# A decoder layer on one Trainium2 core: one projection block earlier in the order, and weight stores on two other queues

## The chip, the cores and the metric

The kernel runs on one core of one Trainium2 chip. The time is that of one execution on the device, in microseconds (us). It is compared between kernels that run on the same chip.

## The reference

One decoder layer, 2048 tokens of width 1024, everything in float32:

```python
h = x @ w_in                       # columns split over three groups of heads
y = [GatedDeltaNet(4 heads of 128) | DilatedWindowAttn(4 heads of 64) | DiffAttn(4 heads)] @ w_out
x = LayerNorm(alpha * x + y)
f = W_down(silu(gate) * val),  [gate, val] = CausalDWConv3(x @ w_up)      # 2752 wide
x = LayerNorm(alpha * x + f)
```

GatedDeltaNet is a linear attention with a state that runs through the tokens in chunks. DilatedWindowAttn is a softmax over three windowed patterns (window 128 at step 1, 512 at step 4, 2048 at step 16), mixed by their log-sums. DiffAttn is full causal attention with two softmax maps, the second subtracted from the first.

## The kernel before, in words

**Products in halves.** TensorE multiplies float32 values as pairs of rounded numbers. Each operand is split into a high part (rounded to the fp32r format) and a low part (the rest), and a product is three matmuls: high by high, high by low, low by high (lines 206 to 208 for the projections, 1158 to 1161 for the products back to model width, 655 to 657 for the values). Moving operands are 512 tokens wide. The tokens are worked in four blocks of 512, numbered 0 to 3.

**Weights.** `Dense.weights` brings one weight tile of 128 by 1024 in two halves of 256 KB. A half that is met for the first time is loaded raw (line 151, tile `wraw`), rounded by ScalarE into `whi` (line 153), and POOL subtracts to get `wlo` (line 154). Where `keep` is set, the two parts of both halves are then stored to device memory (lines 157 to 161, `whi_d` and `wlo_d`), and later uses load those (line 148) and need neither ScalarE nor POOL. `keep` is set by job c0, so the weights of A3, o0 and block 0 of the feed-forward (f0) are stored; those of the gated projections are not. 85 weight tiles are kept: 12 in A3, 8 in o0, 65 in f0, each with four stores.

**Buffers for weights.** Until the end of the second list below, `wraw` has 6 buffers and `whi` and `wlo` 4 each. After it, all three share one ring of 14 tiles (`NW`), so that a raw half takes the slot that a half four or five before it has left.

**Jobs.** The program is written as three lists of jobs, and a job's number is a token block (in i, b, p and r a pair or half of blocks):

- A: projection for the two softmax groups (`Projection.project`: 8 products by `w_att`, then the values by `w_val`, twice over 4 weights; results go to device memory). G: projection for the gated group.
- i, b, p, r: the gated stage. i inverts triangular blocks, b merges them, p prepares keys and queries, r runs the recurrence over two chunks and stores its rows of `y_d`.
- w: dilated window attention of a block. d: differential attention of a block: `stats` (scores, minimum and sum, lines 767 to 776) and `weighted` (lines 818 to 843).
- c0: frees the gated projection's buffers and sets `keep`.
- o0: `Ffn.attend(0)`, the product of `y_d` by `w_out` for block 0 with the first LayerNorm. t0: `Ffn.turn`, which transposes its rows into the moving layout, 8 times 4 transposes (line 1175) and a split.
- f: the feed-forward of a block (`Ffn.block`: 43 products by `w_up`, convolution, products by `w_down`). Within it, attend and turn for the next block are done: attend(1) in f0, attend(2) in f1, attend(3) in f2. So attend(3) needs w3 and d3.

**Order.** A scheduler turns the program into one fixed order for each engine before the run. It simulates the run with a cost model, and each engine takes the ready instruction that stands first in the program. So the place of a job in the lists is its priority, and later jobs fill gaps as far as their buffers are free. On the chip each engine, and each engine's DMA queue, works through its fixed order: an instruction that waits holds up all behind it. Before the change all DMAs are begun on SyncE's queue (SP in the profile).

**Pools.** The second list works with the weight buffers `wp1`, three PSUM banks for products (two `psd`, one `psx`) and five banks of the gated stage; the third list's ring, two more product banks and the four banks for attention scores take the places that these leave. Each block's split tokens `xhi` and `xlo` have 8 buffers in all, one block's worth, so A2, A3 and t0 can't hold theirs at the same time.

Of the kernel before, what the change touches and what calls it, by code (L numbers as in the profile page):

```python
# [27 lines left out]
def cast(x):  # L28
    return x.bitcast(F32)
# [81 lines left out]
class Dense:  # L111
# [15 lines left out]
    def weights(self, src, k=KD, m=P, pool=None, key=None):  # L127


        nc = self.nc  # L130
        n = k // 2 * m
        shape = lambda w: w.rearrange("p (k m) -> p k m", k=k // 2)

        def put(dt, name):
            if pool:
                w = pool.tile([P, TB], dt, tag=name, name=name, bufs=12)
            elif self.ring:
                w = self.wp.tile([P, TB], dt, tag="w", name=name, bufs=self.ring)
            else:
                w = self.wp.tile([P, TB], dt, tag=name, name=name, bufs=NRAW if name == "wraw" else NHALF)  # L140
            return shape(w[:, 0:n])

        his, los = [], []
        for i in range(2):
            if key in self.kept:
                hi, lo = put(F32R, "whi"), put(F32R, "wlo")
                for part, d in zip((hi, lo), self.kept[key]):
                    nc.sync.dma_start(out=cast(part), in_=cast(shape(d[:, i * n : i * n + n])))
            else:
                raw = shape((self.wp.tile([P, TB], F32, tag="w" if self.ring else "wraw", name="wraw", bufs=self.ring or NRAW))[:, 0:n])  # L150
                nc.sync.dma_start(out=raw, in_=src[:, i * (k // 2) : (i + 1) * (k // 2)])
                hi, lo = put(F32R, "whi"), put(F32R, "wlo")
                nc.scalar.copy(hi, raw)  # L153
                nc.gpsimd.tensor_tensor(out=lo, in0=raw, in1=hi, op=ALU.subtract)  # L154
            his.append(hi)
            los.append(lo)
        if key is not None and self.keep and key not in self.kept:
            self.kept[key] = [self.tc.dram_tile([P, 1024], F32R, name=name) for name in ("whi_d", "wlo_d")]
            for parts, d in zip((his, los), self.kept[key]):
                for i in range(2):  # L160
                    nc.sync.dma_start(out=cast(shape(d[:, i * n : i * n + n])), in_=cast(parts[i]))
        return Halves(his), Halves(los)

    def split(self, raw, pool=None, tag="x", bufs=None):
# [1107 lines left out]
def decoder(tc, I, out, y_d=None, upto=3):  # L1272
    nc = tc.nc
    with ExitStack() as ctx:
# [49 lines left out]
        with ExitStack() as second:  # L1324
            dn.ps = Turns(psd, psd, second.enter_context(tc.tile_pool(name="psx", bufs=1, space=PSUM)))
            gdn_phase(tc, I, y_d, dn, gi, SECOND, emit)
        gates.close()
# [5 lines left out]
        ff.open(ctx)  # L1333
        for job in THIRD:
            if job == "f2":
# [36 lines left out]
NZ = 1  # L1372
LAG_PD = 2
FIRST = "A0 G0 A1 G1 d0 w0".split()
SECOND = "i0 b0 p0 b1 p1 r0 b2 p2 r1 G2 b3 p3 r2 G3 c0 i1 r3 p4 p5 b4 b5 r4 b6 r5 A3 p6 p7 b7 r6 r7 o0".split()
THIRD = "w1 d1 A2 t0 d2 w2 w3 d3 f0 f1 f2 f3".split()


def host_arrays(inputs):
# [75 lines left out]
```

## Time and profile before

| | |
|---|---|
| time, median of 3 runs | 3291.5 us (3281.3 to 3293.2) |
| profiled execution: time | 3290.28 us |
| its span | 3288.5 us |
| mean granted TensorE clock | 0.958 |
| device memory read, written | 500.82 MB, 155.39 MB (200 GB/s over the span) |
| stores of `whi_d` and `wlo_d` | 170 and 170, 256 KB each, on SyncE's queue |

The span runs from the first instruction to the last; the execution's own time has 1.8 us around it. In the profile PE is TensorE's matmuls, PEld its weight loads, DVE is VectorE, ACT ScalarE, POOL GpSimd, SP SyncE; a q behind the name is the engine's queue of waits and DMA issues. L161 is line 161 of the kernel. An arrow `out<-in` names the tile written and the tiles read. The granted clock is what the throttle left TensorE, as a share of full speed. The lines of the profile stand in the prediction, where they are used.

### The profile page before, as it was taken

What the parts mean: (1) busy time and instruction counts of PE and PEld (TensorE: products, weight loads), DVE (VectorE), ACT (ScalarE), POOL (GpSimd) and SP (SyncE); (2) the same over time, 40 slices, a digit from 0 to 9 for tenths busy, and PEclk for the clock granted to TensorE, in tenths of its full rate; (3) what the DMA queues carried; (4) which work ended last, traced back from release to release, by engine and by line L of the source; (5) the groups of instructions that cost most, each with busy time, mean ns of one, the idle gap of its engine ahead of it and who ended that gap; (6) DMA issues with size and microseconds to landing.
All of it is one profiled execution on the core that took longest, in us unless ns stands there. A gap on an engine that the chain in (4) does not pass through costs nothing.

```text
span 3288.5 us, 43511 instructions
## 1 busy us (share of the span) xinstructions
PE 3033.3 (92%) x14476; PEld 2318.8 (71%) x14476; DVE 1870.7 (57%) x3392; ACT 1354.4 (41%) x3188; POOL 660.0 (20%) x571
## 2 busy tenths in 40 slices
PE   7898989998597798898899899999999999999998
PEld 5676867786476675565656677778866668888887
DVE  2562759665346245656746675557884444474446
ACT  3653553644144134645744332235653432122213
POOL 4563545442230012242212200000000000000001
PEclk9999989999688898998999999999999999999999
DMA  6546364546797776666677676666874545776554
GB/s 207 168 141 213 121 211 138 156 138 209 247 306 249 240 242 201 199 205 209 203 226 235 215 251 198 183 183 195 261 220 154 162 142 189 243 240 194 192 186 147
DMA packets 474209, 659.29 MB, mean 200 GB/s; under 512 B 75169, under 2 KB 201633, under 8 KB 473217
## 3 DMA queue, kind: packets, MB, share of 16 engines
q1 hardware_dynamic: 473984, 656.52, 63.2%
q8 instruction: 115, 1.88, 0.2%
q14 instruction: 110, 0.89, 0.1%
HBM read 500.82 MB, written 155.39 MB: 200 GB/s over the span
## 4 chain that ended last, share of the span: by engine, by line
PE 56%; DMA 12%; ACT 4%; DVE 3%; issue 2%; SPq 2%; POOL 1%; ACTq 0%; POOLq 0%; DVEq 0%
PE d L208 9%; PE d L206 9%; PE d L207 9%; PE rp L1158 6%; PE rp L1159 6%; PE rp L1161 5%; DMA wraw<-in_w_up 5%; PE bank L818 3%; DMA wraw<-in_w_down 3%; PE bank L833 2%; ACT whi L153 2%; PE bank L997 1%; DMA ks<-fk_d 1%; PE bank L1004 1%; PE bank L767 1%
## 5 line engine op out<-in xcount | busy, mean ns | idle before, releaser
L206 PE MATMUL d<-xhi,whi 128*128 128x512 f32 x2144 | 865.6, 404 | 41.1 <-ACT whi L153 16.4
L208 PE MATMUL d<-xhi,wlo 128*128 128x512 f32 x2144 | 861.3, 402 | 27.8 <-DMA wlo<-wlo_d 14.4
L207 PE MATMUL d<-xlo,whi 128*128 128x512 f32 x2144 | 858.9, 401 | 1.1 <-DVE xlo L169 1.1
L154 POOL TENSOR_TENSOR wlo<-wraw,whi 128x512 fp32r<-128x512 f32 x370 | 504.1, 1367 | 1471.1 <-ACT whi L153 1331.5
L206 PEld LDWEIGHTS d<-xhi,whi 128*128 128x128 f32 x2144 | 412.9, 193 | 153.0 <-ACT whi L153 26.2
L208 PEld LDWEIGHTS d<-xhi,wlo 128*128 128x128 f32 x2144 | 412.0, 192 | 136.8 <-POOL wlo L154 23.3
L207 PEld LDWEIGHTS d<-xlo,whi 128*128 128x128 f32 x2144 | 412.7, 192 | 102.8 <-issue 17.8
L153 ACT CAST whi<-wraw 128x512 fp32r<-128x512 f32 x370 | 227.7, 618 | 390.8 <-DMA wraw<-in_w_up 118.5
L1159 PE MATMUL rp<-wlo,hhi 128*128 128x512 f32 x704 | 280.9, 400 | 2.0 <-POOL wlo L154 2.0
L1158 PE MATMUL rp<-whi,hhi 128*128 128x512 f32 x704 | 268.1, 402 | 12.9 <-ACT whi L153 11.9
L1161 PE MATMUL rp<-whi,hlo 128*128 128x512 f32 x672 | 263.7, 396 | 0.0
L776 ACT ACTIVATE bank<-bank,nm 128x512 f32<-128x512 f32 (+3 forms) x320 | 190.1, 594 | 100.9 <-DVE nm L772 65.2
L1090 ACT COPY ub<-d 128x512 f32<-128x512 f32 x172 | 100.8, 586 | 315.9 <-PE d L208 315.3
L772 DVE TENSOR_REDUCE nm<-bank 128x1 f32<-128x512 f32 (+3 forms) x288 | 164.7, 598 | 96.1 <-PE bank L767 89.6
L843 POOL TENSOR_SCALAR_AFFINE_SELECT pd<-pd 128x128 f32<-128x128 f32 x64 | 32.5, 512 | 854.9 <-DVE pd L839 851.1
L839 DVE SCALAR_TENSOR_TENSOR pd<-pe,f_nlam,pd 128x512 f32<-128x512 f32 (+3 forms) x160 | 124.0, 782 | 138.3 <-ACT pe L835 109.6
L1158 PEld LDWEIGHTS rp<-whi,hhi 128*128 128x128 f32 x704 | 131.7, 189 | 55.4 <-ACT whi L153 19.1
L1159 PEld LDWEIGHTS rp<-wlo,hhi 128*128 128x128 f32 x704 | 133.5, 190 | 39.2 <-issue 6.9
L365 DVE SCALAR_TENSOR_TENSOR yc<-ub,i_taps,yc 128x512 f32<-128x512 f32 x144 | 156.3, 1086 | 3.3
L1168 DVE TENSOR_TENSOR r<-r,rp 128x512 f32<-128x512 f32 x152 | 101.8, 684 | 91.5 <-PE rp L1161 87.0
L1161 PEld LDWEIGHTS rp<-whi,hlo 128*128 128x128 f32 x672 | 127.3, 189 | 31.2 <-issue 4.8
L818 PE MATMUL bank<-pd,fv 128*64 128x512 f32 (+3 forms) x320 | 143.4, 553 | 0.0
(281 smaller groups left out, 4545.7 us busy)
## 6 DMA issues: line engine op xcount, KB each, us to landing
whi<-whi_d SPq DMA_DIRECT2D x486, 256.0 KB
wlo<-wlo_d SPq DMA_DIRECT2D x486, 256.0 KB
whi_d<-whi SPq DMA_DIRECT2D x170, 256.0 KB
wlo_d<-wlo SPq DMA_DIRECT2D x170, 256.0 KB
wraw<-in_w_gdn SPq DMA_DIRECT2D x128, 256.0 KB
ks<-fk_d SPq DMA_DIRECT2D x160, 196.0 KB
wraw<-in_w_up SPq DMA_DIRECT2D x86, 256.0 KB
wraw<-in_w_down SPq DMA_DIRECT2D x50, 256.0 KB
```

What stands on the lines that cost most here:

```text
L153: nc.scalar.copy(hi, raw)
L154: nc.gpsimd.tensor_tensor(out=lo, in0=raw, in1=hi, op=ALU.subtract)
L206: nc.tensor.matmul(out=ps, lhsT=whi[:, k], rhs=xhi[k], start=(k == 0), stop=False)
L207: nc.tensor.matmul(out=ps, lhsT=whi[:, k], rhs=xlo[k], start=False, stop=False)
L208: nc.tensor.matmul(out=ps, lhsT=wlo[:, k], rhs=xhi[k], start=False, stop=(k == KD - 1))
L365: nc.vector.scalar_tensor_tensor(out=yc, in0=ub[:, j : j + TB], scalar=self.taps[:, mt, j : j + 1], in1=yc, op0=ALU.mult, op1=ALU.add)
L772: nc.vector.tensor_reduce(out=o, in_=s[:, 0:nf], axis=mybir.AxisListType.X, op=ALU.min)
L776: nc.scalar.activation(out=s[:, 0:n], in_=s[:, 0:n], func=AF.Exp, scale=-1.0, bias=o, accum_out=den[:, b, m, qt : qt + 1])
L818: nc.tensor.matmul(out=po[64 * hh : 64 * hh + 64, q0:], lhsT=v[:, 64 * hh : 64 * hh + 64], rhs=pd[hh][:, q0:], start=start, stop=stop)
L1158: nc.tensor.matmul(out=ps, lhsT=hi[:, sl], rhs=whi, start=first, stop=False)
L1159: nc.tensor.matmul(out=ps, lhsT=hi[:, sl], rhs=wlo, start=False, stop=last and lo is None)
L1161: nc.tensor.matmul(out=ps, lhsT=lo[:, sl], rhs=whi, start=False, stop=last)
```

## The change

Two edits. In `Dense.weights` the four stores of a kept weight are begun on other queues: the two of the high part on ScalarE's (`nc.scalar`), the two of the low part on POOL's (`nc.gpsimd`). In the lists, A2 moves from the third list, where it stood after w1 and d1, to the second, between r6 and r7; and t0 moves from the third list, where it stood behind A2, to the end of the second, right behind o0. A2 so uses the second list's weight buffers instead of the ring.

```diff
@@ -156,9 +156,9 @@
         if key is not None and self.keep and key not in self.kept:
             self.kept[key] = [self.tc.dram_tile([P, 1024], F32R, name=name) for name in ("whi_d", "wlo_d")]
-            for parts, d in zip((his, los), self.kept[key]):
+            for eng, parts, d in zip((nc.scalar, nc.gpsimd), (his, los), self.kept[key]):
                 for i in range(2):
-                    nc.sync.dma_start(out=cast(shape(d[:, i * n : i * n + n])), in_=cast(parts[i]))
+                    eng.dma_start(out=cast(shape(d[:, i * n : i * n + n])), in_=cast(parts[i]))
         return Halves(his), Halves(los)
@@ -1372,8 +1372,8 @@
 FIRST = "A0 G0 A1 G1 d0 w0".split()
-SECOND = "i0 b0 p0 b1 p1 r0 b2 p2 r1 G2 b3 p3 r2 G3 c0 i1 r3 p4 p5 b4 b5 r4 b6 r5 A3 p6 p7 b7 r6 r7 o0".split()
-THIRD = "w1 d1 A2 t0 d2 w2 w3 d3 f0 f1 f2 f3".split()
+SECOND = "i0 b0 p0 b1 p1 r0 b2 p2 r1 G2 b3 p3 r2 G3 c0 i1 r3 p4 p5 b4 b5 r4 b6 r5 A3 p6 p7 b7 r6 A2 r7 o0 t0".split()
+THIRD = "w1 d1 d2 w2 w3 d3 f0 f1 f2 f3".split()
```

## The prediction

> **What bounds the kernel now.** I read the page first, then the busy time by stages, then in the stage that looked held up the chain of waits and the two lists of waits, and last the timelines of the DMA queue and of TensorE around the moved blocks. The page:
>
> ```profile
> span 3288.5 us, 43511 instructions
> PE 3033.3 (92%) x14476; PEld 2318.8 (71%) x14476; DVE 1870.7 (57%) x3392; ACT 1354.4 (41%) x3188; POOL 660.0 (20%) x571
> ```
>
> TensorE is the bound by this row, but matmuls overlap, so busy says little about pace. The stages show it (us; then busy us and count of each engine, the granted clock, DMA share, GB/s):
>
> ```profile
> 820.00:920.00 100.00, 58.13 (x290) 43.72 (x291) 30.92 (x59) 19.65 (x37) 22.60 (x18) 0.68 0.80 262
> 920.00:1060.00 140.00, 118.09 (x949) 101.29 (x948) 81.47 (x170) 64.84 (x175) 30.03 (x27) 0.91 0.87 279
> 1060.00:1200.00 140.00, 112.69 (x585) 88.32 (x584) 44.17 (x124) 31.70 (x65) 4.63 (x4) 0.88 0.78 246
> 1200.00:1886.00 686.00, 626.32 (x2474) 420.65 (x2473) 418.74 (x764) 362.16 (x865) 194.70 (x164) 0.96 0.67 210
> 1886.00:2714.00 828.00, 824.18 (x3847) 609.63 (x3845) 517.40 (x996) 343.48 (x802) 9.04 (x18) 1.00 0.62 196
> 328.00:410.00 82.00, 81.85 (x435) 65.84 (x434) 58.90 (x95) 40.96 (x89) 42.56 (x34) 1.00 0.39 125
> 3034.00:3116.00 82.00, 82.00 (x363) 67.73 (x362) 37.91 (x57) 16.89 (x43) 0.00 (x0) 1.00 0.60 193
> ```
>
> The last row is the last block's feed-forward alone: 82/363 = 0.226 us for a matmul of 512 columns with nothing in the way. From 1886 on TensorE is full at clock 1.00, and nothing can be won there. The slow part is 820 to 1886: the end of the gated stage with A3 and o0 (to 1060), A2, w1 and t0 (to 1200), and f0 beside d1 and d2 (to 1886). In f0's 686 us, 2474 matmuls at 0.226 would take 559 us. One group is dearer than that price:
>
> ```profile
> L818 PE MATMUL bank<-pd,fv 128*64 128x512 f32 (+3 forms) x160 | 73.2, 554 | 0.0
> ```
>
> It holds TensorE for 73.2 us where 160 x 0.226 = 36 were counted, so the floor is at most 596 us, and about 90 us of f0 are lost. The chain of waits there repeats itself for long stretches (start, us, what):
>
> ```profile
> 1546.89 3.88 DMA wraw<-in_w_down
> ...
> 1550.85 0.63 ACT whi L153
> 1551.48 0.02 issue
> 1551.49 0.32 SPq L161
> 1551.81 0.05 issue
> 1551.86 4.97 DMA wraw<-in_w_down
> ```
>
> A weight half lands, ScalarE rounds it, SyncE's queue, which stood at the store of that half, issues the store, and only then the load of the next half. One load is in flight at a time. The lists of waits over the same 686 us (waiter, what it waited for, us, times, longest), SyncE's and ScalarE's:
>
> ```profile
> SPq L161 <- ACT whi L153: 215.4, 92, 4.5
> SPq L161 <- POOL wlo L154: 46.6, 81, 1.1
> ...
> ACT whi L153 <- DMA wraw<-in_w_up: 118.5, 58, 4.4
> ACT whi L153 <- DMA wraw<-in_w_down: 51.7, 27, 4.3
> ```
>
> 262 us of waiting in front of stores on SyncE, 170 us of ScalarE's waiting for loads. That this is the queue's order and not the weights' path itself, the casts of line 153 show, alone by stage:
>
> ```profile
> 328.00:410.00 82.00, 14.26 (x23) 1.00 0.39 125
> 1200.00:1886.00 686.00, 79.23 (x128) 0.96 0.67 210
> ```
>
> From 328 to 410 the same load, cast and subtract run beside w0, without stores: one half per 3.57 us, TensorE full. In f0 it is one per 5.36 us.
>
> **The stores.** Line 161 issues 4 stores of 256 KB for each kept weight: 12 weights in A3, 8 in o0, 65 in f0, so 340 in all, 260 of them in f0. The change gives 170 to ScalarE's queue and 170 to POOL's.
>
> ```profile
> L161 SPq DMA_DIRECT2D whi_d<-whi x170: 319/320/3069, 745.5 to 1879.6; - x170
> L154 POOL TENSOR_TENSOR wlo<-wraw,whi x370: 1250/1289/3551, 4.5 to 3247.7; 128x512 fp32r<-128x512 f32 x185
> ```
>
> SyncE loses 340 issues (min/median/max in ns, so 0.32 us by the median). In f0 it loses the 262 us of waits too, and the next load then waits only for a slot of the ring of 14 tiles, four halves ahead. ScalarE in f0 gains 130 x 0.32 = 42 us on 362 of 686; the store follows its own cast in program order, so it waits for nobody else, and what queues behind it are the exponentials of d1 and d2. The 170 us that ScalarE now waits for loads cover this; were they gone altogether it would still be busy only 404 of about 600 us. On POOL no DMA issue is in this trace. Bounds: 0.32 us, as on SyncE, and 3.55 us, the slowest POOL operation above. Nothing here lets an issue cost less than nothing. I take 1.3 us, a POOL operation's median: 2.6 us per half with the subtract, below the 3.57 of the rate without stores. The upper end gives 4.8 us per half, and f0 would gain little; both ends stay in the range.
>
> So f0 can gain from 0 to 90 us. The row 328:410 says nearly all, but there the DMA share was 0.39; f0 in 600 us would move 210 x 686/600 = 240 GB/s. I take 60.
>
> A rule of the Trainium skill speaks against this: "DMA: Bandwidth & Descriptors", section "Issuing engines are not separate DMA queues", says that starting DMAs from several engines saves only the sequencer's time of issue, which is usually small. By it f0 would gain one issue per half; the trace disagrees so far as 215 us of waiting stand in front of those issues. Where only issues are dense the rule fits.
>
> **A2 and t0.** A2 is 288 matmuls (65 us at 0.226), and its DMAs are 8 of x, 64 of kept halves and about 45 stores, some 25 MB. They move ahead of r7 and o0 on every queue (SyncE's, the matmuls, ScalarE's and VectorE's copies; POOL has only a memset of it), and no longer stand behind w1 and d1. t0's 32 transposes and 8 splits now follow o0. None of it is cheaper; what counts is which gaps it fills. r7's tail has gaps (TensorE's timeline, with the idle time before each):
>
> ```profile
> 1045.56 1.82 PE L557 MATMUL pk<-S,qk 128*128 128x128 f32 x8 [2.51 <-DVE on L582]
> 1055.22 2.07 PE L564 MATMUL pv<-R,g_xt 128*128 128x128 f32 x8 [7.84 <-DVE R L560]
> ...
> 1070.21 1.12 PE L598 MATMUL yp<-d_ident,on 128*128 128x128 f32 x4 [6.94 <-POOL on L595]
> ```
>
> 17 us in three gaps, which A2 or o0 could fill. But from 820 to 1200 the DMA engines are nearly full: 26.2 + 39.1 + 34.4 = 99.7 MB, which at 279 GB/s, the best stage above, still takes 357 of the 380 us. So this stretch, with its stores moved and its order changed, can gain at most 23 us. It can also lose: A2's 25 MB are 90 us at that rate, put ahead of r7, o0 and so of w1, and SyncE's queue is dense there. Such a stretch, with issues slowed to over a microsecond each by full queues:
>
> ```profile
> 876.43 4.45 SPq L700 DMA_DIRECT2D fk_d<-sy  x3
> 880.98 3.65 SPq L161 DMA_DIRECT2D whi_d<-whi  x2
> ```
>
> I bound it by +40 us lost (A2's 90 less what its own place at 1060 to 1200 frees) and 23 won, and take 20 won, since 80 of the 340 stores leave this queue just here.
>
> **What is late next.** Attention (w1, d1, d2, w2, w3, d3) is one chain of its own. SyncE's timeline gives first loads and last stores of d1, d2 and d3, and the first load of attend(3), which needs d3:
>
> ```profile
> 1273.34 0.86 SPq L741 DMA_DIRECT2D qs<-fq_d  x2
> 1504.63 0.32 SPq L869 DMA_DIRECT2D y_d<-ob  x1
> 1507.27 0.33 SPq L741 DMA_DIRECT2D qs<-fq_d  x1
> 1849.70 0.41 SPq L869 DMA_DIRECT2D y_d<-ob  x1
> 2187.08 0.33 SPq L741 DMA_DIRECT2D qs<-fq_d  x1
> 2713.98 0.32 SPq L869 DMA_DIRECT2D y_d<-ob  x1
> 2825.25 0.32 SPq L1149 DMA_DIRECT2D yraw<-y_d  x1
> ```
>
> d2 took 342 us for 3 key blocks (114 each), d3 527 for 4 (132 each) beside a full TensorE. The slack before attend(3) is 2825 - 2714 = 111 us. If f0 fills TensorE, d1 and d2 slow towards d3's pace; half of the difference, 9 us on 5 blocks, is 45. Then feed-forward can get ahead of attention by only 111 - 45 = 66 us, plus what w1 starts or runs earlier. That allows about 80 us in all, the size of my sum.
>
> **The sum.** 60 + 20 = 80 us from the profiled execution's 3290.3, which lies 1.2 us under the median 3291.5: 3210 us. A difference under 0.5% (16 us) I count as none.
>
> **Rivals.**
> (1) Attention does not bind, because it too runs earlier: 90 + 23 plus some of r7's 17 us, 3290 - 120 = 3170. For it: attention waited for late halves as well in f0's one order of matmuls. Against it: 114 beside 132 us per block.
> (2) Loads stay in a chain, since something else stands before them in SyncE's queue, a slot or a key load; only the store's issue leaves the path: 130 x 0.32 = 42 us, and the early A2 gains nothing: 3250. For it: the full queues at 876. Against it: 215 us of waits at one line. By the Trainium skill's rule above it would come out so.
> (3) The change does not do what it says: the loads are hidden anyway in f0's long stretches with line 818, and A2 only trades places: 3290. Against it: 90 us over the floor.
> (4) Slower: POOL's stores. One POOL issue per half sits between two subtracts on which the third matmul waits. From 5.36 - 1.29 = 4.1 us per issue on, POOL is slower than today's chain; at 4.6 us f0 loses 130 x 0.53 = 69, less the 20 won before it: 3340. For it: nothing hides POOL in f0, and it shares the order. Against it: no POOL row above 3.55 us.
> The Trainium skill has a rule for this: "SBUF — State Buffer", section "SBUF: two separate sides", says that POOL writes the descriptors of its own DMAs and is locked out while VectorE runs certain copies, and its section on the bandwidth-pool intuition gives 0.62 us for such a DMA alone and 3.1 us beside one. No run here shows either; by both, an estimate, POOL would stay under 4.4 us per half.
>
> **How the numbers follow.** Forecast 0.42 (3180 to 3250), rival 1 0.18, rival 2 0.20, rival 3 0.10, rival 4 0.10. Faster by over 0.5% (under 3275): the first three, 0.80. Within: 0.10. Slower: 0.10. The range for 8 in 10 runs from 3140, 30 under rival 1, since f0's floor prices all 2474 matmuls as 512 columns wide and narrower ones are among them, to 3285, which leaves out rival 4 and part of rival 3.
>
> **What would show it.** One more row is the mark for f0's start, its loads of w_up (first and last):
>
> ```profile
> L151 SPq DMA_DIRECT2D wraw<-in_w_up x86: 337/423/775, 1185.1 to 1809.3; - x86
> ```
>
> Right: in f0's chain of waits no store stands between a cast and the next load, and the casts come every 4.5 us or closer; ScalarE's wait for w_up's halves falls below 60 us; A2's matmuls lie ahead of r7's last transposes; the first load of w_up comes before 1185. Attention as the next bound: the first load of attend(3) follows d3's last store by less than 60 us, or TensorE idles there. Wrong: stores on POOL above 3 us each with matmuls of line 208 waiting for wlo; r7's last transposes well past the 1070 above; the casts still 5 us apart.

## The result

The changed kernel takes 3247.3 us (median of 4 runs, 3238.9 to 3252.9), the kernel before 3292.3 us beside it: a ratio of 0.987 [0.985, 0.990], 45 us or 1.3% faster. The forecast was 3210, the range 3140 to 3285. The runs below were made on several chips, each beside the kernel before, whose median there was 3288 to 3292 us; where two kernels are compared closely, their gains over the kernel before beside each are compared, and each gain is good to some 5 to 8 us.

The page of the changed kernel, its span and TensorE's row, then its DMA queues (packets, MB, share of 16 engines):

```profile
span 3251.1 us, 43624 instructions
PE 3017.1 (93%) x14476; PEld 2321.2 (71%) x14476; DVE 1885.6 (58%) x3392; ACT 1359.5 (42%) x3188; POOL 751.3 (23%) x741
...
q1 hardware_dynamic: 425024, 567.36, 55.6%
q10 hardware_dynamic: 24480, 44.58, 3.8%
q0 software_dynamic: 13600, 44.58, 3.6%
```

The stores have left SyncE's queue q1: 44.58 MB go through ScalarE's, as much through POOL's. POOL's busy time rises by 91 us, 170 stores. The line of the stores (ns, min/median/max):

```profile
L161 ACTq DMA_DIRECT2D whi_d<-whi x170: 326/326/378, 744.8 to 1745.0; - x170
L161 POOL DMA_DIRECT2D wlo_d<-wlo x170: 542/559/772, 748.3 to 1746.7; - x170
```

The busy times by stage (us, then busy us and count of each engine, clock, DMA share, GB/s); first the changed kernel:

```profile
820.00:920.00 100.00, 48.69 (x261) 35.95 (x262) 45.02 (x84) 21.67 (x56) 23.31 (x25) 0.71 0.78 246
920.00:1060.00 140.00, 114.86 (x865) 95.17 (x865) 40.27 (x83) 36.85 (x100) 7.14 (x9) 0.89 0.70 214
1060.00:1200.00 140.00, 107.97 (x532) 83.65 (x530) 68.62 (x148) 48.46 (x118) 39.31 (x42) 0.88 0.84 284
1200.00:1700.00 500.00, 481.43 (x2130) 362.36 (x2131) 344.61 (x622) 274.56 (x655) 225.88 (x245) 0.98 0.74 246
```

and the last of these stretches in the kernel before:

```profile
1200.00:1700.00 500.00, 449.80 (x1750) 301.30 (x1749) 303.43 (x593) 281.54 (x705) 148.21 (x121) 0.95 0.65 204
```

From 1200 to 1700 TensorE does 2130 matmuls instead of 1750. In the three stretches ahead it does 261 + 865 + 532 = 1658 where it did 290 + 949 + 585 = 1824 (of mixed shapes): f0 is won, the end of the gated stage is lost.

To add this up, I price each matmul of a trace at the lower quartile of the distance to the next one that its line and shape has in the trace of before, and call what a stretch is longer than its matmuls' prices "lost". In us:

| kernel | to 800 | 800–1200 | 1200–1900 | 1900–2700 | after | all |
|---|---|---|---|---|---|---|
| before | 155 | 155 | 147 | 69 | 2 | 528 |
| changed | 155 | 171 | 76 | 69 | 21 | 492 |
| stores only | 150 | 147 | 67 | 73 | 14 | 451 |
| order only | 148 | 159 | 135 | 68 | 5 | 515 |

528 less 492 is 36, and the two spans differ by 37: +71 in f0's stretch, -16 before it, -19 behind it (between 2700 and 2800).

f0 first. What SyncE's queue and ScalarE wait for in the changed kernel, 1200 to 1700 (waiter, releaser, us, times, longest):

```profile
SPq L151 <- PE d L208: 82.2, 28, 5.4
SPq L736 <- PE bank L767: 68.5, 18, 7.5
```

```profile
ACT whi L153 <- DMA wraw<-in_w_up: 49.3, 29, 6.0
...
ACT whi L153 <- DMA wraw<-in_w_down: 18.7, 14, 2.4
```

SyncE no longer waits in front of line 161; its loads wait for a slot that TensorE must leave. The chain of waits is now TensorE's own for long stretches (start, us):

```profile
1460.09 0.23 PE bank L833
1460.33 0.23 PE d L207
1460.56 0.23 PE d L208
```

The casts alone, 1240 to 1700 (us, busy us and count, clock, DMA share, GB/s), before:

```profile
1240.00:1700.00 460.00, 56.95 (x92) 0.95 0.66 205
```

and changed, with the row of w_up's loads, the mark for f0's start and end:

```profile
1240.00:1700.00 460.00, 64.98 (x105) 0.99 0.75 247
```

```profile
L151 SPq DMA_DIRECT2D wraw<-in_w_up x86: 323/333/855, 1181.4 to 1693.1; - x86
```

One half per 5.0 us became one per 4.4, not one per 3.57 as in the row 328:410 of the prediction, where raw halves had six buffers of their own. f0 begins 4 us earlier than before and loads its last w_up half 116 earlier. What follows the gated stage comes later, though. SyncE's timeline in the changed kernel: d2's first load and last store, d3's, and the first load of attend(3):

```profile
1581.50 0.81 SPq L741 DMA_DIRECT2D qs<-fq_d  x2
2009.88 0.32 SPq L869 DMA_DIRECT2D y_d<-ob  x1
2342.25 0.80 SPq L741 DMA_DIRECT2D qs<-fq_d  x2
2783.66 0.34 SPq L869 DMA_DIRECT2D y_d<-ob  x1
2787.79 0.32 SPq L1149 DMA_DIRECT2D yraw<-y_d  x1
```

d3 ends 70 us later than before (2714), and attend(3) starts 4 us behind it instead of 111.

### The profile page after: what moved, and what is told of

It is laid out like the page before. It is cut to its first block, busy times and chain, and to the rows that moved or that the text cites. A ratio compares the mean times of both kernels' runs of the same rounds, so it can differ in the third digit from the quotient of the medians.

```text
span 3251.1 us, 43624 instructions
## 1 busy us (share of the span) xinstructions
PE 3017.1 (93%) x14476; PEld 2321.2 (71%) x14476; DVE 1885.6 (58%) x3392; ACT 1359.5 (42%) x3188; POOL 751.3 (23%) x741
## 3 DMA queue, kind: packets, MB, share of 16 engines
q10 hardware_dynamic: 24480, 44.58, 3.8%
q0 software_dynamic: 13600, 44.58, 3.6%
## 4 chain that ended last, share of the span: by engine, by line
PE 56%; DMA 4%; DVE 3%; ACT 2%; issue 1%; SPq 0%; POOL 0%; ACTq 0%; DVEq 0%; POOLq 0%
PE d L207 9%; PE d L208 9%; PE d L206 9%; PE rp L1158 6%; PE rp L1159 6%; PE rp L1161 6%; PE bank L818 4%; PE bank L833 2%; PE bank L767 1%; PE bank L997 1%; PE bank L1004 1%; PE bank L958 1%; DMA ks<-fk_d 1%; PE bank L959 1%; DMA wraw<-in_w_up 0%
## 5 line engine op out<-in xcount | busy, mean ns | idle before, releaser
L154 POOL TENSOR_TENSOR wlo<-wraw,whi 128x512 fp32r<-128x512 f32 x370 | 504.8, 1369 | 1095.4 <-ACT whi L153 1014.6
L839 DVE SCALAR_TENSOR_TENSOR pd<-pe,f_nlam,pd 128x512 f32<-128x512 f32 (+3 forms) x160 | 117.0, 737 | 145.7 <-ACT pe L835 111.5
L1095 DVE SCALAR_TENSOR_TENSOR yg<-ub,c_taps,yg 128x512 f32<-128x512 f32 x176 | 145.9, 829 | 3.7
```

The source lines that it names most:

```text
L1095: nc.vector.scalar_tensor_tensor(out=yc, in0=ub[:, j : j + TB], scalar=self.taps[:, mt, j : j + 1], in1=yc, op0=ALU.mult, op1=ALU.add)
```

## The experiments

### The two parts alone

Stores only: the list of jobs of before, the stores on ScalarE's and POOL's queues (the first half of the diff). 

> The stores moved, the lists of jobs as before. Theory A (the gain is the stores' move in f0; the lists' change costs, because A2 delays r7 and with it w1 and all attention by some 65 us, and attention then ends the run): f0's casts come every 4.4 us or closer as in the changed kernel, r7's last transposes lie near 1070 us, w1 starts near 1080, d3's last store lies at 2710 to 2745, and the time is 3195 to 3225 us. Theory B (the order makes the gain, since f0 starts with its tokens ready; the queue of the stores saves no more than the issue time of 0.32 us per half): 3250 us or above, f0's casts still 5 us apart.

Order only: the second half of the diff, all stores on SyncE's queue. 

> The lists of jobs changed, the stores on SyncE's queue as before. Theory A: f0's casts stay 5.2 us or more apart with stores between a cast and the next load, r7's last transposes lie near 1130 us, w1 starts 50 us or more later than before, and the time is 3295 to 3335 us, no faster than before. Theory B: 3240 to 3260 us, like the changed kernel.

Measured: stores only 3217.2 us, ratio 0.977 [0.976, 0.979]; order only 3272.5, 0.994 [0.993, 0.996]. The stores are worth 75 us alone, as theory A had it. The order wins 19 alone, which neither theory of it gave. Together they should have won 94; they won 45. Two questions follow: what about the stores is worth 75 us, and where do the 49 go.

### What about the stores is worth 75 us

Upper halves only and lower halves only, with the list of before:

```diff
-            for parts, d in zip((his, los), self.kept[key]):
+            for eng, parts, d in zip((nc.scalar, nc.sync), (his, los), self.kept[key]):    # upper halves only
+            for eng, parts, d in zip((nc.sync, nc.gpsimd), (his, los), self.kept[key]):    # lower halves only
```

> Order of before; only the upper halves' stores move to ACT's queue, the lower halves' stay on SP. Theory W (what cost time on SP was the wait in it: a store stands there until its half is computed, and the next load behind it): the lower half is computed after the upper one, so SP waits as long as before, on the subtraction instead of the cast: 3275 to 3300 us. Theory I (what cost time is the number of instructions on SP, 0.32 us each, or the stores' place beside the loads): half of the 75 us of both: 3245 to 3262 us.

> Order of before; only the lower halves' stores move to POOL's queue, the upper halves' stay on SP. Theory W: the upper half's store still stands on SP until the cast, 163 us of the waits between 1200 and 1700 us were on that cast and not on the subtraction, so nearly all of them stay, less the 1.5 to 2 us by which the subtraction came later: 3260 to 3300 us. Theory I: half of the 75 us: 3245 to 3262 us.

Measured: upper only 3214.9 us, 0.978 [0.976, 0.980]; lower only 3293.9, 1.001 [1.000, 1.003]. The upper halves alone bring all of it, the lower nothing. Both moves take 170 issues off SyncE, so issue time (theory I) is not the cost. The casts, 1240 to 1700, with upper halves only and then with lower halves only:

```profile
1240.00:1700.00 460.00, 67.55 (x109) 0.99 0.78 252
```

```profile
1240.00:1700.00 460.00, 55.77 (x90) 0.94 0.63 201
```

But theory W falls with the first run too. SyncE's largest wait from 1200 to 1700 with upper halves only:

```profile
SPq L161 <- POOL wlo L154: 218.9, 108, 4.9
```

and the same in the kernel before:

```profile
SPq L161 <- ACT whi L153: 162.8, 71, 4.5
SPq L161 <- POOL wlo L154: 36.6, 64, 1.1
...
SPq L161 <- ACT ub L1089: 21.2, 10, 3.8
SPq L161 <- ACT c_halo L1091: 15.9, 6, 3.3
```

SyncE stands in front of stores nearly as long as before, 219 us against 237, and the kernel is 73 us faster. So this waiting was not the cost by itself. SyncE's timeline before:

```profile
1351.54 0.36 SPq L161 DMA_DIRECT2D whi_d<-whi  x1
1351.96 0.42 SPq L151 DMA_DIRECT2D wraw<-in_w_up  x1
1352.48 0.40 SPq L161 DMA_DIRECT2D wlo_d<-wlo  x1
1354.70 0.34 SPq L736 DMA_DIRECT2D ks<-fk_d  x1
1356.73 0.32 SPq L161 DMA_DIRECT2D whi_d<-whi  x1
1357.10 0.43 SPq L151 DMA_DIRECT2D wraw<-in_w_up  x1
```

and with upper halves only:

```profile
1359.71 0.32 SPq L161 DMA_DIRECT2D wlo_d<-wlo  x1
1360.13 0.38 SPq L736 DMA_DIRECT2D ks<-fk_d  x1
1360.56 0.47 SPq L151 DMA_DIRECT2D wraw<-in_w_down  x1
1362.72 0.32 SPq L161 DMA_DIRECT2D wlo_d<-wlo  x1
1363.10 0.45 SPq L151 DMA_DIRECT2D wraw<-in_w_down  x1
1366.38 0.32 SPq L161 DMA_DIRECT2D wlo_d<-wlo  x1
```

Both alternate store and load, so the difference is which half the store belongs to. Pairing the loads of line 151 with the casts of line 153 in their order, from 1240 to 1650, I counted the loads issued while an earlier half still waited for its cast. Before, there was none for 80 of 83 halves: load, landing, cast, store, and only then the next load. With upper halves only there was one for 61 of 96: the store that the queue stands at belongs to the half before the one in flight. With lower halves only there was none for 78 of 80, with the order only none for 82 of 83, and in the changed kernel at least one for 59 of 94. Theory D therefore: what counts is the number of raw loads in flight, one or two. Three runs tested it, the first two with all stores on ScalarE and POOL, and slots of their own for raw halves from f0 on:

```diff
-tag="w" if self.ring else "wraw", name="wraw", bufs=self.ring or NRAW
+tag="wr" if self.ring else "wraw", name="wraw", bufs=1 if self.ring else NRAW    # NW = 13; two slots: bufs=2, NW = 12
```

> Order of before, all stores on ACT and POOL, but from f0 on the raw weight halves have one slot of their own (the ring keeps 13), so that a load can start only when the half before it has been cast and subtracted. Theory D (what counts is how many raw loads are in flight: before, in 80 of 83 cases none was issued while the one ahead waited for its cast): f0 falls back to 5 us per half and the time to 3275 to 3320 us although no store is left on SP. Theory S (what counts is that SP is rid of the stores): 3210 to 3230 us as with the stores alone.

> The same with two slots for the raw halves (the ring keeps 12): at most two loads in flight. Theory D: two are enough, as with the upper halves alone on ACT: 3205 to 3235 us. If the split of the ring itself costs (fewer slots for the halves), both this and the one with one slot are late by it: over 3240 us.

The third keeps the stores on SyncE, and writes each product's stores one product later (feed-forward only):

```diff
+            def store(his=his, los=los, kept=self.kept[key]): ...    # the four stores
+            self.owed.append(store)    # begun in the next call of weights(), behind its loads
```

> Order of before, all stores on SP's queue as before, but in the feed-forward each product's four stores are written one product later, behind the next product's two loads. Theory D: the loads no longer stand behind the store of the half before them, two or more are in flight, and the time is that of the stores on ACT and POOL: 3205 to 3235 us. Theory S: SP still issues 340 stores and waits in them: 3270 to 3300 us.

Measured: one slot 3329.4 us, 1.012 [1.009, 1.015]; two slots 3238.2, 0.984 [0.981, 0.987]; later stores 3293.1, 1.000 [0.998, 1.002]. With one slot SyncE's largest wait is

```profile
SPq L151 <- POOL wlo L154: 112.9, 68, 2.5
```

that is, the next load waits for the subtraction, with not one store on the queue. The casts, 1240 to 1700, with one slot:

```profile
1240.00:1700.00 460.00, 48.17 (x78) 0.95 0.57 182
```

and with two:

```profile
1240.00:1700.00 460.00, 66.09 (x107) 0.98 0.76 249
```

By the same count as above, with one slot there was no second load in flight for any of 69 halves, with two slots there was one for 87 of 95. One slot more takes the pace from 5.9 to 4.3 us per half and the kernel from 41 us slower than before to 50 faster. This shows theory D, and theory S falls: SyncE rid of its stores is worth nothing while one load is in flight. One slot came out 9 us over its expected range and two slots 3 us; two lose 21 to the stores alone, 11 of them behind 2700 by prices, for which a ring of 12 tiles is a likely cause but not a tested one. The third run did not test what it was for: the later place in the program did not change the fixed order enough, no second load was in flight for 81 of 84 halves, and its time is that of a single load, as D would have it in that case.

### Where the 49 us go

A2 behind r7: `... r6 r7 A2 o0 t0` in place of `... r6 A2 r7 o0 t0`, the rest as changed. 

> The changed kernel with A2 behind r7 instead of ahead of it. If r7 is late because A2 stands ahead of it in the order, its last rows are stored by 1080 to 1105 us instead of 1143, w1 starts 40 us or more earlier, and the time falls to 3205 to 3235 us. If it is late because A2's loads fill the DMA engines and SyncE's queue in that stage whatever their order, the last rows are stored at 1125 or later and the time stays at 3240 to 3255 us.

Of the order only A2's move, t0 back behind d1, stores moved:

```diff
+SECOND = "... b7 r6 A2 r7 o0"
+THIRD = "w1 d1 t0 d2 w2 w3 d3 f0 f1 f2 f3"
```

> Stores moved as in the change, and of the order only A2 is moved into the gated stage; the turn t0 stays behind d1. Theory A2 (with the stores moved it is A2 among the recurrence that costs the 30 us): as the changed kernel, 3235 to 3255 us, r7's last rows near 1140. Theory T (the turn at the end of the stage, ahead of w1, is what costs): 3205 to 3225 us.

The changed kernel with the stores of A3 and o0 back on SyncE:

```diff
+            engs = (nc.sync, nc.sync) if key[0] not in ("up", "down", "end") else (nc.scalar, nc.gpsimd)
+            for eng, parts, d in zip(engs, (his, los), self.kept[key]):
```

> The changed kernel, but the stores of the weight halves of A3, G3's gated weights and o0 (keys gdn, att, val, out) go back to SP's queue; only those of the feed-forward (keys up, down, end) stay on ACT's and POOL's. Tells whether the 50 us that the two parts lose together come from stores on ACT's and POOL's queues inside the gated stage. Theory Q (queues: A3's stores on ACT and POOL stand ahead of the recurrence's operations there and make r5 to r7 late): with them on SP again r7's last rows come near 1104 as in the kernel with the order alone, and the gain of both parts adds up: 3195 to 3215 us. Theory O (order: with A2 ready during the recurrence the fixed order of TensorE is what it is, wherever A3's stores go): r7's last rows stay near 1140 and the time within 10 us of the changed kernel's 3247.

Measured, with the last store of r4's and of r7's rows in the trace (us):

| kernel | time | ratio | r4 | r7 | first load of w1's keys | lost 800–1200 |
|---|---|---|---|---|---|---|
| before | 3288 to 3292 | 1 | 963 | 1079 | 1083 | 155 |
| stores only | 3217.2 | 0.977 [0.976, 0.979] | 955 | 1066 | 1071 | 147 |
| order only | 3272.5 | 0.994 [0.993, 0.996] | 952 | 1104 | 1115 | 159 |
| changed | 3247.3 | 0.987 [0.985, 0.990] | 979 | 1143 | 1157 | 171 |
| A2 behind r7 | 3245.7 | 0.986 [0.985, 0.988] | 972 | 1135 | 1147 | 170 |
| A2 early, t0 late | 3266.5 | 0.994 [0.992, 0.996] | 975 | 1140 | 1152 | 171 |
| A3's and o0's stores on SyncE | 3224.5 | 0.981 [0.979, 0.982] | 954 | 1107 | 1118 | 159 |

A2's place against r7 is without effect. A2's presence in the stage is what costs: with the stores moved it takes the gain over the kernel before from 75 us to 22, and t0 at the end of the stage gives 23 of that back (45). Of the 49 that the parts lose together, 19 are the 80 stores of A3 and o0: with them on SyncE again the gain is 64, r7 ends at 1107 as with the order only, and the time is 3224.5. That is most of theory Q, 10 us short of its range. Without A2 beside them these stores cost nothing: with the stores alone r7 ends at 1066. The trace shows where it starts. From 820 to 920 TensorE has 261 matmuls in the changed kernel (shown above), and with A3's and o0's stores on SyncE

```profile
820.00:920.00 100.00, 60.55 (x346) 46.41 (x349) 31.61 (x68) 16.72 (x34) 18.27 (x15) 0.69 0.84 269
```

346, and r4's rows come 25 us earlier. ScalarE's timeline in the changed kernel shows stores that hold up its other work there:

```profile
857.51 13.66 ACTq L161 DMA_DIRECT2D whi_d<-whi  x3
871.28 0.60 ACT L635 ACTIVATE sy<-d 128x512 fp32r<-128x512 f32 x1 [14.69 <-DMA v<-v_d]
```

The halves of these three stores were cast by 856.6, but the second and third began only at 865.2 and 870.9, each just after a DMA of another job (`fq_d<-sy`, `r<-in_x`) had landed. From 800 to 960 ScalarE's queue stands 43 us in front of line 161, most of it until such a DMA lands, POOL's under 2. With the stores alone ScalarE's queue stands there for 47 us, though, and r7 is early. So these waits are where the stores' cost can lie, but why they cost only with A2 in the stage was not isolated.

The other 30 us are the order's gain of 19, which is gone once f0 is fast, and some 11 more: a gain of 64 against 75 for the stores alone. Alone, the order had f0's first load of w_up come 21 us earlier (before: 1185.1) and its last 22 earlier (1809.3):

```profile
L151 SPq DMA_DIRECT2D wraw<-in_w_up x86: 333/424/1694, 1163.6 to 1787.6; - x86
```

f0 ran at the pace of its chain of loads, so a start 21 us earlier was an end 22 us earlier. With the loads free, f0 waits for TensorE, and the order does not lower what is lost ahead of it (159 against 147 for the stores alone): A2 has left the stretch behind 1060, and r7 and o0 have come into it. This part is read from the traces and not shown by a run of its own: the list of before with only f0's stores moved was not measured, and the kernel with the stores alone has A3's and o0's stores moved too.

### The end of attention

In the changed kernel attend(3) starts 4 us behind d3. Two runs asked whether that sets the time. In the first, attend(3) comes later within f2, `ATT = (17, 18, 20, 99)` for `(17, 18, 18, 99)`. 

> The changed kernel, with attend(3) placed two hidden tiles later in f2 (after tile 20 instead of 18). If attention is the last bound, so that feed-forward runs dry before d3's end, four more products (4 x 24 matmuls x 0.226 = 22 us) can fill TensorE there: the stretch in which it has only lines 818 and 833 shrinks from some 45 us to 25, and the time falls by 8 to 20 us, to 3227 to 3240 us. If the run's end is bound by TensorE alone, nothing moves: 3247 us, 8 us either way.

In the second the last differential block leaves out its first 512 keys in the weighted part:

```diff
-        for b in range(t + 1):
+        b0 = 1 if t == 3 else 0
+        for b in range(b0, t + 1):
```

> The changed kernel, with the weighted part of the last differential block leaving out its first 512 keys (b = 0 of t = 3): some 28% of that block's 64 us at L818 and 48 us at L833, so about 31 us less of TensorE. Theory E (in the changed kernel the last attention block sets when the last feed-forward block can start, and TensorE loses about 20 us beside it between 2700 and 2800 us): the 31 us and most of those 20: 3195 to 3207 us. Rival (TensorE's work alone sets the time): 3212 to 3222 us.

Measured: attend(3) later 3255.2 us, 0.989 [0.987, 0.991], which is 8 slower than the changed kernel and not 8 to 20 faster; it lies at the edge of the other reading, 8 us either way. d3's last store came at 2804 instead of 2784: 96 more matmuls of lines 206 to 208 (22 us at 0.226) stand between 2700 and that store, and d3 moved by about as much. The shorter block: 3220.1 us, 0.979 [0.976, 0.982], 27 less than the changed kernel, or 24 by the gains over the kernel before beside each (69 and 45). By the prices of its matmuls it leaves out 23 us, not the 31 of the expectation, so the rival gives 23 and theory E 23 and most of 20. The run fits the rival; the loss between 2700 and 2800 fell from 20 to 11 us, though. At the most some 10 us hang on attention's end. This stays open, since the profiled execution of the changed kernel is 6 us over its median and that of the shorter one 10 under its.

The best kernels of the study are the stores alone (3217.2) and the upper halves' stores alone (3214.9), both with the list of before; they don't differ by more than their intervals.

## Why the prediction was right, and where it was off

The direction and the mechanism of the larger term were right: one raw load in flight, chained behind its own store. What it got wrong is the other term and the sum of the two. The measured gain is 45 us where 80 were forecast. The sum had neither of the two losses that came (16 in the gated stage, 19 at attention's end). That the time still lies within the forecast's 3180 to 3250 us is in part luck: it lies 3 us from the slow end, and f0's gain of 71 was larger than the 60 it was put at.

- **f0, 60 us.** Right, and a little low: 71 by the table of lost time in the changed kernel, 80 for the stores alone, against a bound of 90. The marks came: no store between cast and load, a cast every 4.4 us (4.5 was named), ScalarE's wait for w_up's halves 49 us up to 1700 (60 was named). But the prediction took the "262 us of waits" of SyncE as the thing that goes. With upper halves only 219 us of such waits stay and the gain is whole. The wait mattered only by where it stood: between a half's cast and the next half's load.
- **POOL's store, 1.3 us between 0.32 and 3.55.** It is 0.56, and 0.77 at the most in the changed kernel. Rival 4 (from 4.1 us on) had no ground. The Trainium skill's "SBUF — State Buffer", section "SBUF: two separate sides", has POOL locked out beside certain VectorE copies, and its section on the bandwidth-pool intuition 3.1 us for such a DMA; with VectorE 69% busy from 1200 to 1700 (344.61 of 500 us) none of the 170 comes near. Whether VectorE ran such copies beside them was not looked at.
- **Rival 2, only the issue leaves the path (3250).** The time came out near 3250, but not for this reason: lower halves only saves as many issues and wins nothing. The Trainium skill's rule ("DMA: Bandwidth & Descriptors", "Issuing engines are not separate DMA queues"), that only issue time is saved, holds for the lower halves: 0 us. For the upper halves it misses 73 us: here an instruction that waits in a queue also decides how many transfers behind it are in flight.
- **The gated stage's end, +20 between +23 and -40.** This step failed. It reckoned gaps that A2 would fill and stores that leave a dense queue; measured, 16 us are lost there (155 to 171). r7's last transposes, which I had named as a mark of "wrong" if well past 1070, begin at 1138, and its last rows are stored at 1143. The stores' leaving, taken as a help "just here", is what costs 19 us when A2 is there too. The reading that a store on ScalarE's queue "waits for nobody else" holds in f0 (0.6 us at most in front of one, 1200 to 1700), but not here, where the queue stands 43 us from 800 to 960. And w1's keys are loaded 74 us later (1157 for 1083), 32 of them with the order alone (1115).
- **The sum.** Taking 60 + 20 as independent was wrong as well. Alone the order was worth 19: f0, bound by its chain of loads, ended 22 us earlier when it started 21 earlier. Beside the free f0 no gain of it is left (64 against 75 for the stores alone); that TensorE's bound takes it away is argued above, not tested.
- **What is late next.** Attention, as named, with the sign named (attend(3) 4 us behind d3, under 60), but its terms were small: d1 and d2 slowed by 125 us (231 to 270 and 342 to 428), not by 45, d1 started 35 later, and d3 took 441 instead of 527. What this costs is 19 us of the table, and the two runs on it did not get them back.

So 3290 - 71 + 16 + 19 = 3254 for the changed kernel's profiled execution (3252.9), where the prediction had 3290 - 60 - 20.

## What to carry to other kernels

Read a long wait in front of a store on a load queue by what stands behind it: count how many loads are in flight while the store waits, since the kernel paid for one instead of two and not for the 200 us of waiting. Two changes that each shorten the same chain-bound stage should not be added: once the first has freed the chain, ask what the second still shortens. And work pulled ahead into the end of another stage can be paid by whatever waits for that end (here w1, 74 us later), so look at that chain's start, not only at the gaps it fills.

## What was not expected of the hardware

A 256 KB store begun on POOL holds POOL 0.54 to 0.77 us (median 0.56), one on ScalarE's queue 0.33, one on SyncE's 0.32 by the medians; the maximum on SyncE, 3.27 us in the kernel before (at 843, in the dense stretch of the gated stage), was not seen on the other two in the changed kernel (0.38 on ScalarE, 0.77 on POOL); over all runs the longest were 1.04 on ScalarE and 1.05 on POOL. The subtraction beside them on POOL kept its mean, 1367 ns before and 1369 after.
